# A two-layer hybrid attention trunk: the forget gate's logarithm as a polynomial, a fourth raw weight buffer and four rotary temporaries

## The chip, the core and the metric

The kernel runs on one core of a Trainium2 chip. The metric is device time in microseconds of one execution; times are medians of several runs. Five engines work side by side, each through its own queue of instructions in a fixed order: PE (TensorE, matrix products), ACT (ScalarE, one input and a function from a table), DVE (VectorE, elementwise work on one or two inputs), POOL (GpSimd, a few elementwise steps here) and SP (SyncE, which here only issues transfers). An instruction waits at the head of its queue until its operands are there, and all behind it waits too.

## What is computed

The reference runs two layers and a last RMSNorm on x of 256 positions by 1024 channels, all in fp32. In a layer:

```python
h = rms_norm(x, gain)
proj = h @ w_in                       # 1024 x 9808, split into the parts below
oa = attention_a(rope(qa), rope(ka), va) * silu(ga)         # causal, 8 heads of 64
isc = sum_h w_idx[h] * relu(rope(q_idx)[h] @ rope(k_idx).T) # the indexer
ob = attention_b(rope(qb), rope(kb), vb, top 64 keys of isc) * silu(gb)
log_f = log_sigmoid(f_logit + f_bias)                       # 256 x 8
oc = attention_c(qc, kc, vc, bias = csum(log_f)[t] - csum(log_f)[s]) * silu(gc)
merged = sum_n sigmoid(merge_n) * (o_n @ w_branch[n])
x = x + merged @ w_out
```

The forget gate's `log_f` is the one place that needs a logarithm: with z the logit plus its bias, log_sigmoid(z) = min(z, 0) - log(1 + exp(-|z|)).

## The kernel before, in words

**Weights and precision.** Each product of weights and activations is made of three passes: every operand is split into a high part `hi` (rounded to fp32r) and a remainder `lo`, and PE adds hi·hi, hi·lo and lo·hi. The weights come raw from memory by a transfer on SP into a `raw` buffer of 128 by 2048 (1 MB in all; `R_RAW` = 3 such buffers). From there ACT writes `wh` (L374) and DVE writes `wl` (L378), in pieces of 128 by 1024, into rings of six. A unit of projection work is 24 products of 128 by 256 into one of three `proj` banks (L419), some units in the other orientation with products 512 wide.

**One layer.** First the value projection, then a unit for the indexer's key and the forget logits (`ev_kwf`, `wf_cols`), four indexer units (`index_scores`), and mixer a, between which stand units of the merge gates (L863). After that mixers c and b with the output products, and the last projection. Each rotated projection goes through `rope` (L465): DVE shuffles into a temporary `rsh` (L468), POOL multiplies it by the sine (L469), DVE multiplies the projection by the cosine into `rr` (L470), and POOL adds (L471). There are two `rsh` and two `rr`. From `rr` ACT writes `qh` (L405), DVE the remainder `qy` (L406), and ACT moves three halves into `qx` and `qy` (L591). Then PE makes the scores in two `s` banks (L604 and L606), ACT takes their relu into `tmp` (L818, L819), and DVE adds them up into `isc` (L827, L829). When all four pairs are in, DVE picks 64 keys per row in eight rounds of `MAX` and `MATCH_REPLACE` (L849, L850).

**The forget gate (`wf_cols`, L758).** PE transposes the logits (L763). DVE makes z and -|z| (L772, L773). ACT takes `Exp` (L777) and then `Ln` of e + 1 (L778); the logarithm needs another function table, so an `ACT_TABLE_LOAD` stands in front of it, and another in front of the next function of the first table, the `Tanh` of L863. Then nine small DVE steps on 128 by 16 elements (L782 to L790) correct the logarithm for small e and give `lf`. PE forms the running sum from `lf` (L796, L797), DVE copies it out (L800 to L803), PE transposes (L808), ACT writes `cT` (L810), and SP loads rows of `cT` into `tmp` (L580). These rows are first used by mixer c (L650).

**What sets the order.** All work is entered as operations with a due key, an engine (sometimes a choice of two), a cost and the buffers it needs. `Plan.run` (L143) then plays the list once with those costs and takes on each engine, among what can start first, the operation with the lowest key; a buffer is taken when an operation starts and given back when its last user is done. So the order on every engine follows from the costs and from how many buffers there are: a change of either moves instructions elsewhere too. The plan gives the `Ln` operation 1540 ns, and an empty ACT operation of 1190 ns stands for the second table load:

```python
def ln():
    ACT.activation(e, na, AF.Exp)
    ACT.activation(u, e, AF.Ln, bias=1.0)
act(ln, 0, False, [], [k_lf], key, "ln", 1540.0)
act(lambda: None, 0, False, [k_lf], [], key - 1, "table", 1190.0)
```

Of the kernel before, what the change touches and what calls it, by code (L numbers as in the profile page):

```python
# [9 lines left out]
F32 = mybir.dt.float32  # L10
F32R = mybir.dt.float32r
AF = mybir.ActivationFunctionType
ALU = mybir.AluOpType

L = 2
S = 256
# [11 lines left out]
NR = {"a": 0, "b": 1, "c": 2}  # L28

C_ID, C_UT, C_MASK, C_ROPE, C_END = 0, 128, 256, 512, 1024  # L30
SWAP = list(range(8, 16)) + list(range(0, 8)) + list(range(16, 32))

R_RING = 6
R_RAW = 3
TAIL = {"ACT": 95.0, "DVE": 85.0, "POOL": 0.0, "PE": 0.0, "SP": 0.0}
STEP = 24.0
SPLIT_LEAD = 2.0
# [206 lines left out]
def hybrid_trunk(ctx, tc, x, norm_gain, w_in, forget_bias, w_branch, w_out, final_gain, consts, out):  # L244
    nc = tc.nc
    PE, ACT, DVE, POOL = nc.tensor, nc.scalar, nc.vector, nc.gpsimd
# [22 lines left out]
    def act(fn, n, ps, reads, writes, key, name="", extra=0.0, touch=(), half=False):  # L269
        o = plan.op([("ACT", t_act(n, ps) + extra, fn)], reads, writes, key, 0.0, name, touch)  # L270
        o.half = half
# [51 lines left out]
    k_id, k_rope, k_gT, k_bdz, k_cst, k_fb, k_wf, k_widx, k_lf, k_cs = (Tok() for _ in range(10))  # L323
# [18 lines left out]
    plan.tag("pth", pts[:1])  # L342
    plan.tag("ptl", pts[1:])
    plan.tag("bd", bd)
    for nm, n, cols, dt in (("rsh", 2, S, F32), ("rr", 2, S, F32),
                            ("th", 2, S, F32), ("g", 4, S, F32), ("e", 4, 384, F32), ("st", 8, 8, F32),
                            ("fb", 2, 384, F32), ("ot", 2, S, F32), ("t8", 4, 8, F32), ("mth", MTH, S, F32)):
        tag(nm, n, [128, cols], dt)
# [409 lines left out]
    def wf_cols(l, key):  # L758
        ps = Buf("t")

        def tr():
            for t in range(2):
                PE.transpose(T(ps)[:, t * 16:t * 16 + 16], wf[64:80, t * 128:(t + 1) * 128], ident[64:80, 64:80])  # L763
        pe(tr, 220.0, [k_wf, k_id], [ps], key, "wf")
        v = lambda: T(ps)[:, :32].rearrange("p (t c) -> p t c", t=2)
        sc = float(np.float32(8 ** -0.5 * 64 ** -0.5))
        dve(lambda: DVE.tensor_scalar(widx, v()[:, :, 0:8], sc, None, op0=ALU.mult), 16, [ps], [k_widx], key, "wf")
        z, na, e, u, c, lf = [fz[:, i].rearrange("p (t c) -> p t c", t=2) for i in range(6)]
        fb = fbias[:, l:l + 1, :].to_broadcast([128, 2, 8])

        def pre():
            DVE.tensor_tensor(z, v()[:, :, 8:16], fb, op=ALU.add)  # L772
            DVE.scalar_tensor_tensor(na, z, -1.0, z, op0=ALU.mult, op1=ALU.min)  # L773
        dve(pre, 0, [ps, k_fb], [k_lf], key, "lf", 300.0)

        def ln():
            ACT.activation(e, na, AF.Exp)  # L777
            ACT.activation(u, e, AF.Ln, bias=1.0)  # L778
        act(ln, 0, False, [], [k_lf], key, "ln", 1540.0)
        act(lambda: None, 0, False, [k_lf], [], key - 1, "table", 1190.0)  # L780

        for f in (lambda: DVE.tensor_scalar(c, e, 1.0, None, op0=ALU.add),  # L782
                  lambda: DVE.tensor_scalar(na, c, 1.0, None, op0=ALU.is_equal),
                  lambda: DVE.tensor_scalar(c, c, -1.0, 5e-8, op0=ALU.add, op1=ALU.max),
                  lambda: DVE.reciprocal(c, c),
                  lambda: DVE.tensor_tensor(c, c, e, op=ALU.mult),
                  lambda: DVE.tensor_tensor(u, u, c, op=ALU.mult),
                  lambda: DVE.tensor_tensor(na, na, e, op=ALU.mult),
                  lambda: DVE.tensor_tensor(u, u, na, op=ALU.add),
                  lambda: DVE.scalar_tensor_tensor(lf, z, 0.0, u, op0=ALU.min, op1=ALU.subtract)):  # L790
            dve(f, 0, [], [k_lf], key + 10, "lf", 100.0, port=True)

        cs = Buf("t")

        def cum():
            PE.matmul(T(cs)[:, :16], ut, lf.rearrange("p t c -> p (t c)"), start=True, stop=False)  # L796
            PE.matmul(T(cs)[:, 8:16], ones, lf[:, 0], start=False, stop=True)  # L797
        pe(cum, 400.0, [k_lf, k_cst], [cs], key + 10, "csum", MARGIN)
        w = lambda: T(cs)[:, :16].rearrange("p (t c) -> p t c", t=2)
        dve(lambda: DVE.tensor_copy(csum, w()), 16, [cs], [k_cs], key, "csum")  # L800
        dve(lambda: DVE.tensor_scalar(ncs, w(), -1.0, None, op0=ALU.mult), 16, [cs], [k_cs], key, "csum")
        rep, k_rep = wf.rearrange("p (t r c) -> p t r c", t=2, r=16), Tok()
        dve(lambda: DVE.tensor_copy(rep, w().unsqueeze(2).to_broadcast([128, 2, 16, 8])), S, [cs], [k_rep, k_wf], key + 10, "csum")  # L803
        pt = Buf("t")

        def tr2():
            for t in range(2):
                PE.transpose(T(pt)[:, t * 128:(t + 1) * 128], wf[:, t * 128:(t + 1) * 128], ident)  # L808
        pe(tr2, 225.0, [k_rep, k_id], [pt], key + 10, "cT", MARGIN)
        act(lambda: ACT.activation(cT, T(pt)[:, :S], AF.Copy), S, True, [pt], [k_rep, k_cT], key + 10, "cT")  # L810
# [306 lines left out]
```

## Time and profile before

| | |
|---|---|
| median of 3 runs | 618.05 us (617.97 to 618.89) |
| the profiled execution | 618.74 us |
| its span, first to last instruction | 616.9 us |
| TensorE clock granted | 0.997 of full speed |
| PE / DVE / ACT / POOL busy | 98% / 87% / 73% / 15% of the span |
| moved by transfers | 107.32 MB, mean 174 GB/s |

The span is shorter than the profiled execution by 1.8 us. Times in rows are in us from the span's start. In a row of the timeline the first number is the start and the second the duration; what stands in brackets is the idle time before it and what ended that. Matmuls are pipelined: one lasts 0.28 us, but the next starts 0.11 us after it, so waits of PE are read from the distance between starts and not from its busy share. In a table of stretches each row gives the stretch, its length, and the busy time of PE, its weight loads (PEld), DVE, ACT and POOL with the number of instructions, then the clock, the busy share of the transfer engines and GB/s.

### The profile page before, as it was taken

Reading aid. Unit: us, or ns where it says so; the run is one execution under the profiler, and the core shown is the slowest. Engines: PE = TensorE matmul, PEld = TensorE weight load, DVE = VectorE, ACT = ScalarE, POOL = GpSimd, SP = SyncE. Lnnn points to the kernel's source line nnn. Section 1 sums busy time; section 2 is a strip of 40 time slices with the busy share of each in tenths; the row PEclk is TensorE's granted clock in tenths of the full one; section 3 lists DMA queues with packets and bytes.
Section 4 is the critical chain, followed back from the end, with each engine's and each line's share of the span. In section 5 each row is a group of like instructions: output and inputs, shape, how many; then the busy total and the mean of one; then the engine's idle time right before and its main releaser. Section 6 shows DMA issues by size and latency. Waiting matters only on the chain.

```text
span 616.9 us, 12615 instructions
## 1 busy us (share of the span) xinstructions
PE 606.5 (98%) x4804; PEld 581.1 (94%) x4804; DVE 534.5 (87%) x1322; ACT 451.7 (73%) x948; POOL 95.0 (15%) x101
## 2 busy tenths in 40 slices
PE   8999999999999999999999999999999999999995
PEld 6899999999998999999889999998999989999985
DVE  7899999985998889988588999998678988999773
ACT  5788398876996778775587866997688766987541
POOL 1251242000000233200006305300000013220001
PEclk9999999999999999999999999999999999999998
DMA  8962765655554563575555639455637365453711
GB/s 283 304 195 90 226 171 191 200 171 172 171 173 136 180 197 99 175 237 173 158 170 174 204 114 276 141 170 185 209 103 231 112 201 157 155 169 122 257 35 69
DMA packets 96156, 107.32 MB, mean 174 GB/s; under 512 B 4576, under 2 KB 84832, under 8 KB 96096
## 3 DMA queue, kind: packets, MB, share of 16 engines
q1 hardware_dynamic: 95808, 106.13, 54.7%
q8 instruction: 37, 0.61, 0.4%
q10 hardware_dynamic: 288, 0.39, 0.2%
q14 instruction: 23, 0.19, 0.1%
HBM read 103.37 MB, written 1.05 MB: 169 GB/s over the span
## 4 chain that ended last, share of the span: by engine, by line
PE 78%; DVE 13%; ACT 4%; issue 2%; DMA 1%; POOL 1%; SPq 0%; POOLq 0%; DVEq 0%; ACTq 0%
PE proj L419 68%; DVE wl L378 5%; PE t L692 3%; DVE isc L850 2%; PE proj L996 1%; PE s L604 1%; PE s L606 1%; DVE t L849 1%; DMA x<-in_x_dram 1%; DVE isc L829 1%; DVE rsh L468 1%; ACT wh L374 1%; PE o L708 1%; PE o L711 1%; DVE rr L470 1%
## 5 line engine op out<-in xcount | busy, mean ns | idle before, releaser
L419 PE MATMUL proj<-hTh,wh 128*128 128x256 f32 (+1 forms) x1040 | 270.1, 278 | 0.0
L419 PE MATMUL proj<-hTl,wh 128*128 128x256 f32 (+1 forms) x1040 | 269.7, 277 | 0.0
L378 DVE TENSOR_TENSOR wl<-raw,wh 128x1024 fp32r<-128x1024 f32 (+1 forms) x190 | 235.5, 1248 | 38.3 <-ACT wh L374 37.7
L374 ACT ACTIVATE wh<-raw 128x1024 fp32r<-128x1024 f32 (+1 forms) x190 | 199.0, 1053 | 51.1 <-PE proj L419 41.3
L419 PE MATMUL proj<-hTh,wl 128*128 128x256 f32 (+1 forms) x1040 | 234.0, 278 | 0.0
L419 PEld LDWEIGHTS proj<-hTh,wh 128*128 128x128 f32 (+1 forms) x1040 | 194.7, 187 | 0.2
L419 PEld LDWEIGHTS proj<-hTl,wh 128*128 128x128 f32 (+1 forms) x1040 | 194.6, 187 | 0.3
L419 PEld LDWEIGHTS proj<-hTh,wl 128*128 128x128 f32 (+1 forms) x1040 | 175.6, 187 | 0.0
L469 POOL TENSOR_TENSOR rsh<-rsh,cst 128x256 f32<-128x256 f32 (+1 forms) x42 | 35.6, 849 | 351.9 <-DVE rsh L468 351.7
L471 POOL TENSOR_TENSOR rr<-rr,rsh 128x256 f32<-128x256 f32 (+1 forms) x42 | 51.1, 1220 | 8.2 <-DVE rr L470 5.4
L669 ACT ACTIVATE e<-e,st 128x128 f32<-128x128 f32 x96 | 42.7, 446 | 6.9 <-DVE st L665 6.6
L419 PE MATMUL proj<-wh,v 128*128 128x512 f32 (+1 forms) x144 | 35.5, 368 | 0.0
L419 PE MATMUL proj<-og0l,wh 128*128 128x256 f32 x128 | 33.9, 277 | 0.0
L419 PE MATMUL proj<-og0h,wh 128*128 128x256 f32 x128 | 32.4, 278 | 0.0
L419 PE MATMUL proj<-wh,hTh 128*128 128x512 f32 x80 | 32.4, 405 | 0.0
L419 PE MATMUL proj<-wh,hTl 128*128 128x512 f32 x80 | 31.5, 393 | 0.0
L419 PEld LDWEIGHTS proj<-wh,v 128*128 128x128 f32 x144 | 25.2, 188 | 4.7
L419 PE MATMUL proj<-og0h,wl 128*128 128x256 f32 x128 | 28.6, 277 | 0.0
L697 DVE TENSOR_TENSOR ptl<-t,pth 128x384 fp32r<-128x384 f32 x48 | 24.9, 551 | 0.6 <-ACT pth L695 0.6
L419 PE MATMUL proj<-wl,hTh 128*128 128x512 f32 x80 | 24.9, 392 | 0.0
L419 PEld LDWEIGHTS proj<-og0h,wh 128*128 128x128 f32 x128 | 24.0, 188 | 0.0
L419 PEld LDWEIGHTS proj<-og0l,wh 128*128 128x128 f32 x128 | 24.0, 188 | 0.0
(194 smaller groups left out, 1046.1 us busy)
## 6 DMA issues: line engine op xcount, KB each, us to landing
raw<-in_w_in_dram SPq DMA_DIRECT2D x74, 1024.0 KB, 5.3
raw<-in_w_branch_dram SPq DMA_DIRECT2D x24, 512.0 KB, 3.5
raw<-in_w_out_dram SPq DMA_DIRECT2D x8, 1024.0 KB, 6.9
tmp<-wf SPq DMA_DIRECT2D x16, 128.0 KB, 5.2
raw<-in_w_in_dram SPq DMA_DIRECT2D x3, 512.0 KB, 7.9
x<-in_x_dram SPq DMA_DIRECT2D x4, 256.0 KB, 5.1
raw<-in_w_in_dram SPq DMA_DIRECT2D x2, 320.0 KB, 6.0
out_dram<-tmp SPq DMA_DIRECT2D x2, 320.0 KB, 2.5
```

The lines of the kernel that those rows point to most:

```text
L374: ACT.activation(p[0].v, sel(c.v), AF.Copy)
L378: DVE.tensor_tensor(p[1].v, sel(c.v), p[0].v.bitcast(F32), op=ALU.subtract)
L419: PE.matmul(o(), a(), b(), start=first and i == 0, stop=last and i == n - 1)
L468: dve(lambda: DVE.stream_shuffle(T(sh)[:np_], a(), SWAP), S, [ps], [sh], key, "rope")
L469: gps(lambda: POOL.tensor_tensor(T(sh)[:np_], T(sh)[:np_], s[:np_], op=ALU.mult), S, [k_rope], [sh], key, "rope")
L470: dve(lambda: DVE.tensor_tensor(T(r)[:np_], a(), c[:np_], op=ALU.mult), S, [ps, k_rope], [r], key, "rope")
L471: gps(lambda: POOL.tensor_tensor(T(r)[:np_], T(r)[:np_], T(sh)[:np_], op=ALU.add), S, [sh], [r], key, "rope")
L604: PE.matmul(o.rearrange("p (h c) -> p h c", h=2), qh[:, sl], kl[:, :, :n], start=True, stop=False)
L669: act(lambda t=t, a=a, n=n, e=e, st=st: ACT.activation(T(e)[:, a:a + n], T(e)[:, a:a + n], AF.Exp, bias=T(st)[:, t:t + 1], scale=-1.0, acc ...
L692: PE.transpose(T(ps)[:, i * 128:(i + 1) * 128], T(es[h])[:, i * 128:(i + 1) * 128], ident)
L697: dve(lambda h=h, src=src: DVE.tensor_tensor(T(pl)[:, h], src(), T(ph)[:, h].bitcast(F32), op=ALU.subtract), 384, [ps, kp[h][0]], [kp[h][1 ...
L850: dve(lambda o=o, t8=t8: DVE.match_replace(o, T(t8), o, TAKEN), n, [t8], [k_isc[i]], key + r * step, "top8")
```

## The change

Four things are changed.

1. The logarithm is no longer taken by ACT. With s = e / (e + 2), log(1 + e) = 2 atanh(s), and DVE works out a polynomial in s² with five coefficients: ten steps on 128 by 16 elements (L780 to L789 of the changed kernel) stand for nine. ACT keeps `Exp` alone. The `Ln`, the table load in front of it and the table load behind it go, and so does the plan's empty operation for it.
2. `R_RAW` is 4 and no longer 3.
3. There are four `rsh` and four `rr`, no longer two of each.
4. The room for these, 8 KB and 4 KB per partition, comes from the memory set aside for descriptors of transfers that POOL would issue (`dynamic_dma_scratch_size=1024`); this kernel issues none from POOL.

```diff
+ATANH = (2.0, 0.666663146821, 0.400249102795, 0.279606027472, 0.281783350867)
-R_RAW = 3
+R_RAW = 4
-    for nm, n, cols, dt in (("rsh", 2, S, F32), ("rr", 2, S, F32),
+    for nm, n, cols, dt in (("rsh", 4, S, F32), ("rr", 4, S, F32),
-        def ln():
-            ACT.activation(e, na, AF.Exp)
-            ACT.activation(u, e, AF.Ln, bias=1.0)
-        act(ln, 0, False, [], [k_lf], key, "ln", 1540.0)
-        act(lambda: None, 0, False, [k_lf], [], key - 1, "table", 1190.0)
-
-        for f in (lambda: DVE.tensor_scalar(c, e, 1.0, None, op0=ALU.add),
-                  lambda: DVE.tensor_scalar(na, c, 1.0, None, op0=ALU.is_equal),
-                  lambda: DVE.tensor_scalar(c, c, -1.0, 5e-8, op0=ALU.add, op1=ALU.max),
-                  lambda: DVE.reciprocal(c, c),
-                  lambda: DVE.tensor_tensor(c, c, e, op=ALU.mult),
-                  lambda: DVE.tensor_tensor(u, u, c, op=ALU.mult),
-                  lambda: DVE.tensor_tensor(na, na, e, op=ALU.mult),
-                  lambda: DVE.tensor_tensor(u, u, na, op=ALU.add),
-                  lambda: DVE.scalar_tensor_tensor(lf, z, 0.0, u, op0=ALU.min, op1=ALU.subtract)):
+        act(lambda: ACT.activation(e, na, AF.Exp), 16, False, [], [k_lf], key, "lf")
+
+        s, s2, q = na, c, u
+        for f in (lambda: DVE.tensor_scalar(s2, e, 2.0, None, op0=ALU.add),
+                  lambda: DVE.reciprocal(s2, s2),
+                  lambda: DVE.tensor_tensor(s, e, s2, op=ALU.mult),
+                  lambda: DVE.tensor_tensor(s2, s, s, op=ALU.mult),
+                  lambda: DVE.tensor_scalar(q, s2, ATANH[4], ATANH[3], op0=ALU.mult, op1=ALU.add),
+                  lambda: DVE.tensor_tensor(q, q, s2, op=ALU.mult),
+                  lambda: DVE.scalar_tensor_tensor(q, q, ATANH[2], s2, op0=ALU.add, op1=ALU.mult),
+                  lambda: DVE.scalar_tensor_tensor(q, q, ATANH[1], s2, op0=ALU.add, op1=ALU.mult),
+                  lambda: DVE.scalar_tensor_tensor(q, q, ATANH[0], s, op0=ALU.add, op1=ALU.mult),
+                  lambda: DVE.scalar_tensor_tensor(lf, z, 0.0, q, op0=ALU.min, op1=ALU.subtract)):
             dve(f, 0, [], [k_lf], key + 10, "lf", 100.0, port=True)
...
-    nc = _bacc.Bacc("TRN2", target_bir_lowering=False, num_devices=1)
+    nc = _bacc.Bacc("TRN2", target_bir_lowering=False, num_devices=1, dynamic_dma_scratch_size=1024)
```

Since costs and buffers change, the plan moves instructions on every engine. PE has the same 4145 rows, and they stand as before except in the first part of each layer: rows 169 to about 890, and 2283 to about 2890 (the indexer, mixer a and the start of mixer c). There blocks of 6 to 48 projection products change places with scores, transposes and weighted sums. On SP three raw loads now stand ahead of the first load of `cT` rows in layer 1 that stood behind it, and in layer 2 single row loads stand one or two raw loads later.

ACT in layer 1, from the forget gate's exponential on. Before (`rr` is the rotary sum, `qh` the high part made from it, `acc` the first merge gate):

```order
L777 ACTIVATE fz<-fz 128x16
L778 ACT_TABLE_LOAD
L778 ACTIVATE fz<-fz 128x16
L744 ACTIVATE bd0h<-rr_123 64x256
L374 ACTIVATE wh_68<-raw_118 128x1024
L405 ACTIVATE qh_80<-rr_124 128x256
L374 ACTIVATE wh_63<-raw_118 128x1024
L374 ACTIVATE wh_64<-raw_119 128x1024
L405 ACTIVATE qh_81<-rr_123 128x256
L746 ACTIVATE bd0h<-bd0h 64x256
```

ACT at the same place, after the change:

```order
L777 ACTIVATE fz<-fz 128x16
L745 ACTIVATE bd0h<-rr_126 64x256
L375 ACTIVATE wh_68<-raw_120 128x1024
L375 ACTIVATE wh_63<-raw_120 128x1024
L747 ACTIVATE bd0h<-bd0h 64x256
L406 ACTIVATE qh_80<-rr_127 128x256
L375 ACTIVATE wh_64<-raw_121 128x1024
L592 ACTIVATE qx_83<-qh_80 64x256
L406 ACTIVATE qh_81<-rr_128 128x256
L375 ACTIVATE wh_65<-raw_121 128x1024
L406 ACTIVATE qh_82<-rr_129 128x256
```

The table load and the `Ln` are gone, the rotary sums lie in four buffers (126 to 129) where they lay in two (123, 124), and the three `qh` stand closer together, each still waiting for POOL at the head of ACT's queue. Further down the second table load, ahead of the first `acc`, is gone too.

PE in layer 1 at the indexer's third score (buffers `qh_82`, `qx_85`, `qy_88`). Before:

```order
L419 MATMUL proj_160<-hTl,wh_63 128x256
L419 MATMUL proj_160<-hTh,wl_70 128x256
L419 MATMUL proj_160<-hTh,wh_63 128x256
L419 MATMUL proj_160<-hTl,wh_63 128x256
L419 MATMUL proj_160<-hTh,wh_63 128x256
L419 MATMUL proj_160<-hTh,wl_70 128x256
L419 MATMUL proj_160<-hTl,wh_63 128x256
L604 MATMUL s_162<-bd0l,qh_82 128x256
```

PE at the same place, after the change:

```order
L420 MATMUL proj_165<-hTl,wh_63 128x256
L605 MATMUL s_167<-bd0l,qh_82 128x256
L607 MATMUL s_167<-bd0h,qx_85 128x128
L607 MATMUL s_167<-bd0h,qy_88 128x128
L605 MATMUL s_168<-bd0l,qh_82 128x512
L607 MATMUL s_168<-bd0h,qx_85 128x256
L607 MATMUL s_168<-bd0h,qy_88 128x256
L420 MATMUL proj_165<-hTh,wl_70 128x256
```

The score now stands six products earlier. In layer 1 the first score stands 12 products later, and the running sum of the forget gate 42 later. In layer 2 the third score stands 6 later and the fourth 6 earlier, and the running sum 12 later. The first weighted sum of mixer a in layer 1 stands 6 earlier.

DVE in layer 2 at the end of the forget gate's small steps (`fz`), among the selection rounds. Before:

```order
L789 TENSOR_TENSOR fz<-fz 128x16
L850 MATCH_REPLACE isc<-t_148,isc 128x256
L790 SCALAR_TENSOR_TENSOR fz<-fz 128x16
L378 TENSOR_TENSOR wl_71<-raw_119,wh_64 128x1024
L800 COPY csum<-t_164 128x16
```

DVE at the same place, after the change:

```order
L787 SCALAR_TENSOR_TENSOR fz<-fz 128x16
L849 MATCH_REPLACE isc<-t_153,isc 128x256
L788 SCALAR_TENSOR_TENSOR fz<-fz 128x16
L379 TENSOR_TENSOR wl_70<-raw_118,wh_63 128x1024
L634 SCALAR_TENSOR_TENSOR g_132<-th_130,proj_165 128x256
L789 SCALAR_TENSOR_TENSOR fz<-fz 128x16
L379 TENSOR_TENSOR wl_71<-raw_118,wh_64 128x1024
```

The last `fz` step, for which PE's running sum waits, now stands behind a weight remainder and a gate product of mixer a.

## The prediction

> **What bounds the kernel now.** First the span and the table of stretches, cut where the work of a layer changes: the first part of layer 1, its rest, the first part of layer 2.
>
> ```profile
> span 616.9 us, 12615 instructions
> 31.00:131.00 100.00, 99.45 (x814) 96.10 (x813) 96.60 (x261) 78.60 (x164) 24.49 (x24) 1.00 0.58 181
> 131.00:329.00 198.00, 198.00 (x1547) 188.97 (x1547) 166.20 (x385) 145.07 (x304) 20.25 (x22) 1.00 0.55 173
> 329.00:425.00 96.00, 95.32 (x793) 92.63 (x792) 90.05 (x255) 76.60 (x166) 25.80 (x25) 1.00 0.56 171
> ```
>
> From 131 to 329 PE is busy for every microsecond at full clock. In the two first parts PE is short of that by under 1 us, but DVE is busy for 96.60 of 100 us and 90.05 of 96, and ACT for less than 80%. So the kernel is bound by PE's products, and only in the two first parts does another engine hold PE up. The chain that ended last says the same in shares:
>
> ```profile
> PE 78%; DVE 13%; ACT 4%; issue 2%; DMA 1%; POOL 1%; SPq 0%; POOLq 0%; DVEq 0%; ACTq 0%
> ```
>
> The same chain in order of time, one long piece of projection work, which gives PE's pace:
>
> ```profile
> 128.23 24.52 PE proj L419 x216
> ```
>
> 216 products in 24.52 us are 0.1135 us each. PE's busy share hides short waits, since a product lasts 0.28 us and the next starts after 0.11 us. So I read PE's timeline for starts that lie further apart than that. Here are the seven widest places in the two first parts, with the fourth score of layer 1 (50.90 to 51.29) as the yardstick without a wait:
>
> ```profile
> 47.99 0.28 PE L419 MATMUL proj<-hTl,wh 128*128 128x256 f32 x1
> 48.42 0.27 PE L606 MATMUL s<-bd0h,qy 128*128 128x128 f32 x1
> 49.06 0.50 PE L604 MATMUL s<-bd0l,qh 128*128 128x512 f32 x1 [0.37 <-ACT tmp L819]
> 50.90 0.28 PE L419 MATMUL proj<-hTh,wl 128*128 128x256 f32 x1
> 51.18 0.28 PE L606 MATMUL s<-bd0h,qy 128*128 128x128 f32 x1
> 51.29 0.45 PE L604 MATMUL s<-bd0l,qh 128*128 128x512 f32 x1
> 60.59 0.28 PE L419 MATMUL proj<-hTl,wh 128*128 128x256 f32 x1
> 60.90 0.40 PE L796 MATMUL t<-fz,cst 128*128 128x16 f32 x2
> 85.91 0.28 PE L606 MATMUL s<-bd2h,qy 128*128 128x128 f32 x1
> 86.25 0.50 PE L604 MATMUL s<-bd2l,qh 128*128 128x512 f32 x1
> 98.47 0.28 PE L419 MATMUL proj<-hTl,wh 128*128 128x256 f32 x1
> 98.84 0.36 PE L708 MATMUL o<-pth,v 128*128 128x256 f32 x1
> 340.79 0.28 PE L606 MATMUL s<-bd1h,qy 128*128 128x128 f32 x1
> 341.14 0.50 PE L604 MATMUL s<-bd1l,qh 128*128 128x512 f32 x1
> 345.24 0.22 PE L606 MATMUL s<-bd1h,qx 128*128 128x128 f32 x1
> 345.39 0.33 PE L606 MATMUL s<-bd1h,qy 128*128 128x128 f32 x1
> 345.87 0.50 PE L604 MATMUL s<-bd1l,qh 128*128 128x512 f32 x1
> 360.82 0.28 PE L419 MATMUL proj<-hTl,wh 128*128 128x256 f32 x1
> 361.50 0.40 PE L796 MATMUL t<-fz,cst 128*128 128x16 f32 x2 [0.41 <-DVE fz L790]
> ```
>
> Layer 1: the third score takes 1.07 us from 47.99 to 49.06 against 0.39 on the yardstick, so it waits 0.68; the running sum 0.31 less 0.11, 0.20; the score at 86.25 0.34 less 0.11, 0.23; the weighted sum at 98.84 0.37 less 0.11, 0.26. Layer 2: the second score 0.35 less 0.11, 0.24; the third 0.15 less 0.06 and 0.48 less 0.11, 0.46; the running sum 0.68 less 0.11, 0.57. That is 2.64 us. I take 0.05 more for each restart, since the step after 49.06 is somewhat wider than after 51.29, and so 3.0 us. This is all that a change to order and helpers in these parts can win: 0.5%.
>
> **The change part by part.**
>
> *The table loads.* Two go in each layer.
>
> ```profile
> L778 ACT ACT_TABLE_LOAD x2 | 2.6, 1283 | 0.0
> L863 ACT ACT_TABLE_LOAD x2 | 2.6, 1283 | 0.0
> ```
>
> Two pieces of the chain in order of time, in layer 2:
>
> ```profile
> 341.69 1.28 ACT L863
> 345.34 0.49 ACT tmp L819
> ```
>
> ACT is freed of 2 x 1.28 us and the `Ln` per layer, about 2.7 us. ACT is not what bounds the span, so this counts only where ACT is late for PE. In the chain's order of time the second load of layer 2 (341.69) stands on the chain, ahead of the relu at 345.34 that empties the score bank for the third score. Its 1.28 us are more than the 0.46 that this score waits, and the score stands 6 products (0.68 us) later now. I count the 0.46 whole, between 0 and 0.46. The second score (0.24) lies ahead of that load; only the load after the exponential is out of its way, and there ACT then waits for POOL, so I count 0.14, from 0 to 0.24.
>
> On the cost of a switch, the row says 1.28 us, and the next ACT instruction of the timeline follows at once. The Trainium skill (ScalarE: Activation LUTs, What ACT_TABLE_LOAD costs) puts a drain of about 1.38 us on top, 2.66 us per switch in all; the trace does not agree, since no such gap stands in it, but by that figure ACT would be freed of about 5.3 us per layer.
>
> *The third score of layer 1* now stands 6 products earlier, so PE is there 0.68 us sooner, and the 0.68 that it waited become 1.36 unless ACT comes sooner too. ACT is freed of 2.7 us, but not all arrives: its three `qh` stand at the head of its queue waiting for rotary sums, and POOL now takes the third multiplication ahead of the second sum.
>
> ```profile
> 334.39 0.80 POOL L471 TENSOR_TENSOR rr<-rr,rsh 128x256 f32<-128x256 f32 x1
> 336.94 1.60 POOL L471 TENSOR_TENSOR rr<-rr,rsh 128x256 f32<-128x256 f32 x1
> ```
>
> A sum takes 0.80 or 1.60 us on POOL (layer 2 has both), so one step put ahead delays the second `qh` by 0.8 to 1.6 us. That leaves 1.1 to 1.9 us of the 2.7. I take 1.1, since DVE is nearly always busy here and the longer sum is the usual one in this part; of the 1.36 us some 0.26 remain, and about 0.4 of the 0.68 is won. Bounds: all of it, or -0.68 if nothing arrives.
>
> *The logarithm on DVE.* Ten steps stand for nine per layer.
>
> ```profile
> 45.94 0.17 DVE L782 TENSOR_SCALAR fz<-fz 128x16 f32<-128x16 f32 x1
> 46.14 0.17 DVE L783 TENSOR_SCALAR fz<-fz 128x16 f32<-128x16 f32 x1
> 59.98 0.17 DVE L788 TENSOR_TENSOR fz<-fz 128x16 f32<-128x16 f32 x1
> 60.07 0.29 DVE L849 MAX8 t<-isc 128x8 f32<-128x128 f32 x1
> 361.28 0.16 DVE L790 SCALAR_TENSOR_TENSOR fz<-fz 128x16 f32<-128x16 f32 x1
> 361.36 1.22 DVE L378 TENSOR_TENSOR wl<-raw,wh 128x1024 fp32r<-128x1024 f32 x1
> ```
>
> Two steps behind each other that depend on each other start 0.20 apart (45.94, 46.14); one followed by other work takes 0.09 (59.98, 60.07). In layer 1 six of the nine stood in one row, 6 x 0.20 + 3 x 0.09 = 1.5 us; now nearly all ten stand between other steps, 10 x 0.09 = 0.9. So DVE gains 0.6 us there, and in layer 2, where the nine were partly spread, about nothing; ends, 0.9 saved and 0.5 lost. DVE is nearly always busy, so this is worth having, but the two waits that I ascribe to DVE's pace in mixer a (86.25 and 98.84) come closer as well when PE comes sooner. I count 0 of their 0.49, between -0.5 and +0.49.
>
> *The running sums.* In layer 1 it stands 42 products later, 4.77 us, behind which DVE has some 3.8 us more to do by the rows of the order; the 0.20 goes. In layer 2 it stands 12 later, 1.36 us, but its last `fz` step stands behind a remainder more (1.22) and a gate product (0.3), so DVE must come some 0.7 us sooner than now to keep the wait from growing. I take half of 0.57 as won, 0.28, between -0.5 and +0.57.
>
> *The buffers.* The fourth raw buffer is costed at nothing, and so is the room taken from POOL's descriptors, which no transfer here uses.
>
> ```profile
> ACT wh L374 <- DMA raw<-in_w_in_dram: 6.1, 5, 2.8
> 64.42 1.27 SPq L580 DMA_DIRECT2D tmp<-wf  x2
> 106.33 1.40 DVE L650 SCALAR_TENSOR_TENSOR fb<-tmp,ncs,cst 128x128 f32<-128x128 f32 x4
> ```
>
> ACT waited for raw weights 6.1 us in all, while PE had a ring of six pieces to work on, so no wait of PE goes with it; without that ring up to 2.8 us would show. The row loads for mixer c go out behind three more raw loads on SP's queue, but they left at 64.42 and are first used at 106.33, some 40 us of cover.
>
> *Moved work.* Elsewhere in mixer a blocks change places. Most scores and sums come later, which gives their operands time; the first weighted sum of layer 1 and the fourth score of layer 2 come 6 products earlier. I put 0.2 us against it, from 0 to 1.4.
>
> Sum: 0.46 + 0.14 + 0.40 + 0.20 + 0.28 - 0.20 = 1.28 us, and 0.05 for each of two restarts that go, 1.4 us. The span becomes 615.5 and the profiled execution 617.3; that one lay 0.7 above the median of 618.05, so the median becomes 616.7 us.
>
> **The rivals.**
>
> *Everything clears* (chance 0.17). All seven waits go: 618.05 - 3.0 = 615.0 us. For it: most of the places stand later now. Against: the two at DVE's pace.
>
> *DVE holds the pace* (0.25). ACT's freed time turns into idle time of ACT, PE meets fewer waits at the scores and longer ones at the transposes and weighted sums of mixer a, and the first parts last as long as before: 618.0 us. For it: DVE at 96.60 of 100. Against: in layer 2 DVE has about 6 us of idle time in 96, part of it behind ACT.
>
> *PE comes too soon* (0.14). Four operands come no sooner than before: those of the third score and the first weighted sum in layer 1, of the fourth score in layer 2, and the last `fz` step of layer 2. Three places 6 products earlier cost 0.68 each, the fourth 0.2 more; with 0.46 and 0.20 won at the places that moved back, 618.05 + 2.2 - 0.7 = 619.6 us. It decides where ACT's `qh` come less than 0.68 us sooner; for it, that they wait for POOL at the head of the queue.
>
> *The longer switch* (0.04). If a switch takes ACT longer than its load, twice the time is freed, the third score of layer 1 clears wholly, and so does the second of layer 2: 616.7 - 0.28 - 0.10, 616.3 us. This is what the skill's drain would do; the trace gives no sign of it.
>
> **How the numbers follow.** The forecast has 0.40. A measurement of this kernel tells about 0.2%, 1.24 us, from no change, so faster means below 616.8 and slower above 619.3. The forecast lies almost at that line: 0.25 of it on the faster side, 0.15 on the other. Faster: 0.25 + 0.17 + 0.04 = 0.46. Same: 0.15 + 0.24 of the second rival + 0.02 of the third = 0.41. Slower: 0.12 + 0.01 = 0.13. The range goes from 614.9, just below all waits gone, to 619.0: beyond it lie most of the third rival and a little below, 0.18 together.
>
> **What would show it.** Right: no table load but the first; the relu L819 ahead of the third score of layer 2 at least 0.5 us sooner; starts 0.11 apart at the places of 49.06, 60.90 and 345.87; the stretch of layer 2's first part shorter by 0.7 to 1 us, that of layer 1 by 0.4 to 0.8, and the long middle stretch unchanged. Wrong: the waits found again, as wide, at the transposes (L692) and weighted sums (L708); `qh` waiting longer for POOL; the running sum of layer 2 waiting over 0.6; or a part of the gain or loss outside the first parts of the layers, in the first 31 us above all, where the fourth raw load now leaves earlier beside the others.

## The result, and the profile after

The changed kernel takes 615.07 us (median of 5 runs) against 618.05 us before (5 runs): a ratio of 0.9944, with a 95% interval from 0.9928 to 0.996. It is faster by 3.0 us, about 0.5%. The prediction said 616.7: the gain is more than twice the forecast's 1.4 us. The number is that of the rival in which all seven waits go, 615.0; that it fits to a tenth is in part luck, as the fixed points below show.

The first profile of the changed kernel fell in an execution whose clock was low all through (0.655, a span of 862.4 us), so the profile shown is of another run of the same kernel, `after_again` below. Its span, the stretches that the prediction used, and the shares of the chain that ended last:

```profile
span 612.9 us, 12602 instructions
31.00:131.00 100.00, 100.00 (x829) 97.45 (x828) 96.96 (x263) 79.20 (x168) 21.84 (x24) 1.00 0.58 178
131.00:329.00 198.00, 198.00 (x1547) 188.97 (x1547) 166.89 (x387) 143.60 (x302) 22.13 (x24) 1.00 0.56 176
329.00:425.00 96.00, 96.00 (x793) 93.27 (x792) 93.25 (x259) 75.37 (x161) 22.61 (x24) 1.00 0.57 173
PE 97%; DVE 1%; issue 1%; ACT 0%; POOL 0%; POOLq 0%
```

PE is now busy for every microsecond of the two first parts, where 0.55 and 0.68 us were missing, and within the same 100 us it gets through 829 instructions instead of 814. The chain is PE's at 97% instead of 78%; the 13% that went through DVE are down to 1%, the 4% through ACT to 0%. The middle stretch is as it was. Of ACT's table loads one is left in the whole program:

```profile
L502 ACT ACT_TABLE_LOAD x1 | 1.3, 1283 | 3.6 <-DMA x<-in_x_dram 3.6
```

PE's timeline at three of the seven places: the third score of layer 1 (47.09, the row 512 wide), and the running sums of layer 1 (64.16) and layer 2 (359.26).

```profile
46.98 0.28 PE L607 MATMUL s<-bd0h,qy 128*128 128x128 f32 x1
47.09 0.45 PE L605 MATMUL s<-bd0l,qh 128*128 128x512 f32 x1
...
64.04 0.28 PE L420 MATMUL proj<-hTh,wl 128*128 128x256 f32 x1
64.16 0.29 PE L795 MATMUL t<-fz,cst 128*128 128x16 f32 x2
...
359.14 0.28 PE L420 MATMUL proj<-hTl,wh 128*128 128x256 f32 x1
359.26 0.29 PE L795 MATMUL t<-fz,cst 128*128 128x16 f32 x2
```

Each starts 0.11 or 0.12 us after the row ahead of it; before it was 0.64, 0.31 and 0.68. No wait stands at the other four places either.

To say in which layer the time came, I measure between fixed points. PE transposes the forget logits once in each layer; between these two rows lie all of layer 1's first part and its rest, and from the second to the end of the span lies layer 2. Before:

```profile
27.01 0.29 PE L763 MATMUL t<-cst,wf 16*128 16x16 f32 x2
```

The second such row of before starts at 326.49, those of the changed kernel at 26.43 and 324.24. With spans of 616.94 and 612.89 us, layer 1 goes from 299.48 to 297.81 us (1.67 less), layer 2 from 290.45 to 288.65 (1.80 less), 3.5 us together. The remaining 0.6 of the 4.0 us between the two spans lies ahead of the first transpose and is the profiled execution of before alone: the profiles of all twelve kernels in the table below, that of `poly_old_order` among them, which has before's order, start that row between 26.02 and 26.59.

Over all executions the median span falls by 3.8 us (616.7 for before beside `after_again`, 612.9 for the changed kernel), but the time by only 3.4. The changed kernel spends 2.1 to 2.2 us outside its span in each of its ten executions, and every other kernel of this study 1.7 to 1.9. These 0.35 us are a loss that the prediction did not have, and no run shows what they are; `poly_only` and `buffers_only` have none of it.

### The profile page after: what moved, and what is told of

Its sections match the earlier page's. It is cut to its first block, busy times and chain, and to the rows that moved or that the text cites. A ratio compares the mean times of both kernels' runs of the same rounds, so it can differ in the third digit from the quotient of the medians.

```text
span 862.4 us, 12602 instructions
## 1 busy us (share of the span) xinstructions
PE 854.8 (99%) x4804; PEld 795.8 (92%) x4804; DVE 549.3 (64%) x1324; ACT 454.7 (53%) x941; POOL 90.4 (10%) x102
## 4 chain that ended last, share of the span: by engine, by line
PE 97%; DVE 1%; issue 1%; DMA 0%; POOL 0%; ACT 0%; POOLq 0%; DVEq 0%
PE proj L420 85%; PE t L693 3%; PE s L607 2%; PE s L605 2%; PE proj L995 1%; PE o L709 1%; PE o L712 1%; PE o L710 0%; PE o L711 0%; DMA x<-in_x_dram 0%; PE t L521 0%; PE s L521 0%; DVE wl L987 0%; DVE wh L985 0%; DVE hTl L535 0%
## 5 line engine op out<-in xcount | busy, mean ns | idle before, releaser
L420 PE MATMUL proj<-hTh,wh 128*128 128x256 f32 (+1 forms) x1040 | 349.8, 345 | 0.0
L420 PE MATMUL proj<-hTl,wh 128*128 128x256 f32 (+1 forms) x1040 | 349.3, 344 | 0.0
L420 PE MATMUL proj<-hTh,wl 128*128 128x256 f32 (+1 forms) x1040 | 306.1, 343 | 0.0
L420 PEld LDWEIGHTS proj<-hTl,wh 128*128 128x128 f32 (+1 forms) x1040 | 257.9, 248 | 0.9 <-issue 0.2
L420 PEld LDWEIGHTS proj<-hTh,wh 128*128 128x128 f32 (+1 forms) x1040 | 255.5, 246 | 1.2
L420 PEld LDWEIGHTS proj<-hTh,wl 128*128 128x128 f32 (+1 forms) x1040 | 235.1, 249 | 0.4
L420 PE MATMUL proj<-wh,v 128*128 128x512 f32 (+1 forms) x144 | 48.3, 468 | 0.0
L420 PE MATMUL proj<-og0h,wh 128*128 128x256 f32 x128 | 42.7, 346 | 0.0
L865 ACT ACTIVATE mth<-proj 128x256 f32<-128x256 f32 x32 | 12.3, 383 | 48.5 <-PE proj L420 48.4
L696 ACT ACTIVATE pth<-t 128x384 fp32r<-128x384 f32 x48 | 22.9, 491 | 21.0 <-PE t L693 20.7
```

The source lines that it names most:

```text
L420: PE.matmul(o(), a(), b(), start=first and i == 0, stop=last and i == n - 1)
L696: act(lambda h=h, src=src: ACT.activation(T(ph)[:, h], src(), AF.Copy), 384, True, [ps], [kp[h][0]], key, "pT", touch=[ph])
L865: act(lambda: ACT.activation(T(th), T(ps)[:, :S], AF.Tanh, scale=0.5), S, True, [ps], [th], u - EARLY, "mth")
```

## The experiments

Two theories stood against each other at first. **A**: PE waited for what the two table loads of a layer kept ACT from doing; the order and the buffers matter little. **B**: the new order and the additional buffers removed the waits. All times are medians in us; ratios are to before, run on the same chip beside them (618.47, 618.32 and 618.40 us for the first four kernels, the next four and the last four), with 95% intervals.

| kernel | us | ratio |
|---|---|---|
| `after_again` | 615.04 | 0.9945 (0.9932 to 0.9957) |
| `poly_only` | 615.60 | 0.9953 (0.9940 to 0.9966) |
| `poly_old_order` | 615.40 | 0.9949 (0.9935 to 0.9963) |
| `buffers_only` | 617.14 | 0.9978 (0.9969 to 0.9987) |
| `loads_back` | 618.43 | 1.0003 (0.9994 to 1.0012) |
| `fill_exp` | 615.75 | 0.9961 (0.9948 to 0.9973) |
| `fill_gate` | 618.48 | 1.0000 (0.9992 to 1.0009) |
| `dve_tax` | 621.12 | 1.0050 (1.0037 to 1.0062) |
| `tanh_early` | 616.27 | 0.9963 (0.9950 to 0.9977) |
| `buffers_tanh` | 615.93 | 0.9960 (0.9947 to 0.9972) |
| `poly_raw` | 615.14 | 0.9946 (0.9934 to 0.9958) |
| `poly_temps` | 614.56 | 0.9937 (0.9924 to 0.9949) |

The second table is PE's timeline read as in the prediction: the distance of a start from the one ahead of it, less the pace (0.113 us behind a product 256 wide, 0.06 behind one 128 wide). The seven columns are the places of the prediction: in layer 1 (1) the third score, the running sum, a score and a weighted sum of mixer a, in layer 2 (2) the second score, the third, and the running sum. A dash is less than 0.14 us. These are single distances, so they differ from the prediction's by up to 0.1.

| kernel | 1 third | 1 sum | 1 score a | 1 weighted | 2 second | 2 third | 2 sum |
|---|---|---|---|---|---|---|---|
| before | 0.58 | 0.20 | 0.28 | 0.26 | 0.29 | 0.42 | 0.57 |
| `loads_back` | 0.58 | 0.19 | 0.29 | 0.22 | 0.29 | 0.42 | 0.68 |
| `fill_gate` | 0.59 | 0.17 | 0.28 | 0.17 | - | 0.34 | 0.71 |
| `fill_exp` | - | - | 0.27 | 0.17 | - | - | - |
| `poly_old_order` | - | - | - | 0.18 | - | - | - |
| `tanh_early` | - | - | - | 0.17 | 0.58 | - | - |
| `buffers_only` | - | - | - | - | 0.29 | 0.42 | 0.61 |
| `after_again` | - | - | - | - | - | - | - |

### The parts by themselves

`after_again` is the changed kernel unaltered. `poly_only` has its polynomial with before's numbers of buffers:

```diff
-R_RAW = 4
+R_RAW = 3
-    for nm, n, cols, dt in (("rsh", 4, S, F32), ("rr", 4, S, F32),
+    for nm, n, cols, dt in (("rsh", 2, S, F32), ("rr", 2, S, F32),
```

`buffers_only` is before with the four numbers of the change and its logarithm on ACT kept:

```diff
-R_RAW = 3
+R_RAW = 4
-    for nm, n, cols, dt in (("rsh", 2, S, F32), ("rr", 2, S, F32),
+    for nm, n, cols, dt in (("rsh", 4, S, F32), ("rr", 4, S, F32),
-    nc = _bacc.Bacc("TRN2", target_bir_lowering=False, num_devices=1)
+    nc = _bacc.Bacc("TRN2", target_bir_lowering=False, num_devices=1, dynamic_dma_scratch_size=1024)
```

`poly_old_order` is before with the polynomial in place of the logarithm and nothing else changed: the plan is told the old costs, and two of the ten steps are entered as one operation, so that PE, POOL and SP run word for word in before's order, and ACT does but for the `Ln` and the two loads:

```diff
         def ln():
             ACT.activation(e, na, AF.Exp)
-            ACT.activation(u, e, AF.Ln, bias=1.0)
         act(ln, 0, False, [], [k_lf], key, "ln", 1540.0)
         act(lambda: None, 0, False, [k_lf], [], key - 1, "table", 1190.0)
-        for f in (lambda: DVE.tensor_scalar(c, e, 1.0, None, op0=ALU.add),
...
+        def first():
+            DVE.tensor_scalar(s2, e, 2.0, None, op0=ALU.add)
+            DVE.reciprocal(s2, s2)
+        for f in (first,
+                  lambda: DVE.tensor_tensor(s, e, s2, op=ALU.mult),
...
```

> The changed kernel itself, for a profile at full clock. If all seven waits of the forecast went (the rival in which everything clears), the first part of layer 1 is shorter by 1.3 to 1.5 us and that of layer 2 by 1.3 to 1.5, with starts 0.11 us apart at every one of the seven places; time 0.995 of the kernel before. If the forecast's sum was right part by part and something outside those parts gave the rest, the two first parts are shorter by 1.4 us together, and 1.5 us lie elsewhere, most likely in the first 31 us, where the fourth raw load leaves earlier.

> The polynomial and the plan's new costs, with three raw buffers and two temporaries of each kind as before. Theory A (the time of the table loads on ScalarE is what PE waited for, buffers matter little): faster by 2 to 3 us, ratio 0.995 to 0.997. Theory B (the new order and the buffers that allow it are what clears the waits): faster by 0 to 1 us, ratio 0.998 to 1.000.

> The fourth raw buffer and the four temporaries, with the logarithm from ScalarE's table as before. Theory A: the table loads are still there, so faster by 0.5 us at most, ratio 0.999 to 1.000. Theory B: faster by 1.5 to 2.5 us, ratio 0.996 to 0.998. If PE comes too soon at places moved forward, slower by up to 1 us.

> The polynomial in the order of the kernel before: the plan is given the old costs (the 1540 and the empty 1190 ns) and nine operations for the ten steps, buffers as before, so every instruction stands as it stood and only the Ln and the two table loads per layer are missing. Theory A: faster by 1.5 to 2.5 us, ratio 0.996 to 0.9975, with the waits of layer 1's third score and layer 2's second and third score gone and those of the running sums left. Theory B: faster by under 1 us, ratio 0.9985 to 1.000.

The polynomial alone gives 615.6 us in the order that the plan makes of it and 615.4 in before's own, 2.9 and 3.1 us of the 3.4 that the whole change gives. The old order loses all seven waits but one. Theory A had expected less of it, 1.5 to 2.5 us, with the waits of the running sums left; these go too, and why is shown below. So the order isn't the main cause, and theory B falls as the main one. The buffers alone still give 1.3 us, more than theory A allowed and less than theory B. All of it is in layer 1, which is 1.46 us shorter between the fixed points, while layer 2 is 0.46 longer: they relieve the waits of layer 1 in another way, and so the two gains do not add up.

The order does clear one place that the prediction did not list, because it lies inside a merged row. In layer 2 the second of three transposes of mixer a (387.52 in before) starts 0.32 us after the first, where 0.11 is usual. Every kernel in before's order keeps this wait of 0.2 us, `poly_old_order` too; the changed kernel does not have it.

### Which of the loads, and by what

What of the polynomial was it: the `Ln` no longer waited for, the first load, or the second? `loads_back` puts the instructions back on ACT in `poly_old_order`, but the result of the `Ln` goes to a place that the last small step overwrites, so that it is not used:

```diff
             ACT.activation(e, na, AF.Exp)
+            ACT.activation(lf, e, AF.Ln, bias=1.0)
```

`fill_exp` and `fill_gate` put one idle copy each in the place of one load, behind the exponential or ahead of the layer's first merge gate (`fill` is a buffer of its own that nobody reads):

```diff
             ACT.activation(e, na, AF.Exp)
+            ACT.activation(fill, ident[:, :1].to_broadcast([128, 1280]), AF.Copy)
```

```diff
+            def gate():
+                if late:
+                    late.pop()
+                    ACT.activation(fill, ident[:, :1].to_broadcast([128, 1280]), AF.Copy)
+                ACT.activation(acc[:, j], T(ps)[:, :S], AF.Tanh, scale=0.5)
```

> The polynomial in the order of before, with ScalarE's Ln put back although nobody reads its result: it is written where the last small step writes later. So both table loads of a layer and the Ln come back at their old places on ScalarE, while VectorE keeps the polynomial, which does not wait for the Ln. poly_old_order took 615.4 us, before 618.5. Theory A (PE waited for what the loads kept ScalarE from doing): all of it is lost again, 617.8 to 618.6 us, with PE's waits back at the third score of layer 1 (0.5 us or more) and at the third score of layer 2 (0.4 or more). Rival B (VectorE gained, because its steps no longer wait for a logarithm and stand less in a row): it stays within 0.5 us of 615.4.

> The polynomial in the order of before, with one ScalarE copy of 128 by 1280 (an estimated 1.28 us, by 1056 ns for 1024 columns) right behind the forget gate's exponential, at the place of the first table load; nothing reads it. Theory A as the prediction had it (behind the exponential ScalarE waits for POOL's rotary sums anyway, so the first load mostly fills a wait): 615.4 to 616.0 us. Rival C (ScalarE is in debt through this whole part, so each load costs the same wherever it stands): half of the 3 us, 616.6 to 617.2.

> The polynomial in the order of before, with the same copy of 128 by 1280 on ScalarE in front of the first merge gate of each layer, at the place of the second table load. Theory A as the prediction had it (the second load stands right ahead of the relus for the third score): most of the 3 us comes back, 617.0 to 618.0 us, with the third scores of both layers waiting again. Rival C (each load costs the same): 616.6 to 617.2, as fill_exp.

`loads_back` is before again, in its time and in all seven waits: the gain is ACT's time and nothing that the polynomial does on DVE. And the two loads are not alike. The copy in the first place costs 0.35 us, which the two intervals do not tell from nothing; between the fixed points it is 0.35 in layer 1, where the score of mixer a waits again, and nothing in layer 2. The copy in the second place costs 3.1 us, all of the gain and more than theory A expected. Rival C, the same cost anywhere, falls.

The reason for the first stands on ACT's timeline of layer 1. `poly_old_order` behind its exponential (27.37):

```profile
27.37 0.21 ACT L778 ACTIVATE fz<-fz 128x16 f32<-128x16 f32 x1
29.10 0.42 ACT L745 ACTIVATE bd0h<-rr 64x256 fp32r<-64x256 f32 x1 [1.51 <-POOL rr L472]
```

`fill_exp` there:

```profile
27.81 0.21 ACT L780 ACTIVATE fz<-fz 128x16 f32<-128x16 f32 x1
27.93 1.26 ACT L781 ACTIVATE fill<-cst 128x1280 f32<-128x1280 f32 x1
29.54 0.42 ACT L747 ACTIVATE bd0h<-rr 64x256 fp32r<-64x256 f32 x1 [0.35 <-POOL rr L474]
```

ACT has a hole of 1.51 us there, in which it waits for POOL's rotary sum, and 1.26 us of copy fit into it: the hole becomes 0.35. The second load meets no hole. Before, layer 1:

```profile
40.11 1.28 ACT L863 ACT_TABLE_LOAD   x1
41.41 0.38 ACT L863 ACTIVATE acc<-proj 128x256 f32<-128x256 f32 x1
41.69 1.06 ACT L374 ACTIVATE wh<-raw 128x1024 fp32r<-128x1024 f32 x1
42.64 0.37 ACT L818 ACTIVATE tmp<-s 128x256 f32<-128x256 f32 x1
42.90 0.42 ACT L405 ACTIVATE qh<-rr 128x256 fp32r<-128x256 f32 x1
...
46.76 1.05 ACT L374 ACTIVATE wh<-raw 128x1024 fp32r<-128x1024 f32 x1
47.71 0.37 ACT L818 ACTIVATE tmp<-s 128x256 f32<-128x256 f32 x1
48.11 0.41 ACT L591 ACTIVATE qy<-qh 64x256 fp32r<-64x256 f32 x1
48.43 0.57 ACT L819 ACTIVATE tmp<-s 128x512 f32<-128x512 f32 x1
```

From the load to the relu at 48.43, which empties the score bank for PE's third score (49.06), no row has a bracket: ACT never waits, and so the 1.28 us arrive there whole. `fill_gate` has the same picture with a copy, and PE's third score behind it waits for the same relu:

```profile
39.38 1.25 ACT L874 ACTIVATE fill<-cst 128x1280 f32<-128x1280 f32 x1
40.66 0.39 ACT L875 ACTIVATE acc<-proj 128x256 f32<-128x256 f32 x1
```

```profile
47.66 0.28 PE L609 MATMUL s<-bd0h,qy 128*128 128x128 f32 x1
48.31 0.50 PE L607 MATMUL s<-bd0l,qh 128*128 128x512 f32 x1 [0.37 <-ACT tmp L827]
```

Behind the same load DVE waits too, and this is the part that I had not seen. DVE's timeline of before, all of its waits from 38 to 62 and from 338 to 362:

```profile
43.35 0.42 DVE L406 TENSOR_TENSOR qy<-rr,qh 128x256 fp32r<-128x256 f32 x1 [0.73 <-ACT qh L405]
47.85 1.23 DVE L378 TENSOR_TENSOR wl<-raw,wh 128x1024 fp32r<-128x1024 f32 x1 [0.61 <-ACT wh L374]
...
343.71 0.43 DVE L406 TENSOR_TENSOR qy<-rr,qh 128x256 fp32r<-128x256 f32 x1 [0.23 <-ACT qh L405]
344.65 1.22 DVE L378 TENSOR_TENSOR wl<-raw,wh 128x1024 fp32r<-128x1024 f32 x1 [0.52 <-ACT wh L374]
348.09 1.23 DVE L378 TENSOR_TENSOR wl<-raw,wh 128x1024 fp32r<-128x1024 f32 x1 [0.60 <-ACT wh L374]
```

That is 1.34 us in layer 1 and 1.35 in layer 2, each time behind a `qh` or `wh` that follows the load on ACT (in layer 1 those at 42.90 and 46.76 above). In `poly_old_order` no row of DVE in these two windows has a bracket; in `fill_gate` there are 0.98 and 0.83 us again. Behind them DVE has no wait of 0.1 us or more up to 100 in layer 1 and up to 390 in layer 2, so it carries the delay on to the running sum, for which PE waits 0.57 us in layer 2, and to the score of mixer a in layer 1, which `fill_gate` brings back (0.28).

### Is DVE the pace?

`dve_tax` adds two products to DVE in each layer of `poly_old_order`, behind the second and the sixth small step:

```diff
             DVE.reciprocal(s2, s2)
+            DVE.tensor_tensor(fill[:, :1024], ident[:, :1].to_broadcast([128, 1024]), ident[:, :1].to_broadcast([128, 1024]), op=ALU.mult)
...
             DVE.tensor_tensor(q, q, s2, op=ALU.mult)
+            DVE.tensor_tensor(fill[:, :1024], ident[:, :1].to_broadcast([128, 1024]), ident[:, :1].to_broadcast([128, 1024]), op=ALU.mult)
```

> The polynomial in the order of before, with two more VectorE products of 128 by 1024 in each layer, behind the second and behind the sixth small step; nobody reads them. By the rows of the weight remainders 1.22 us each, 2.4 us per layer, about as much as ScalarE lost with the loads. If VectorE sets PE's pace in the first part of layer 1 (97 of 100 us busy), what it has to do more shows in full there, 2.4 us, and in part in layer 2: 618 to 620 us. If its waits were ScalarE's in the main, it has room: 615.4 to 616.5.

With 621.12 us it lies above both expectations. Against `poly_old_order` it costs 5.7 us, more than the 4.7 that the products take (two groups of 2.4 and 2.3 us). Between the fixed points layer 1 is 3.02 us longer than in `poly_old_order` and layer 2 2.03. In layer 2 that is nearly the 2.4 us of DVE work, and it shows as one wait: the running sum starts 2.01 us after the product ahead of it. In layer 1 the same sum starts 1.68 us after it, so some 0.8 of the 2.4 us were absorbed, but a slower clock was added, which the last section shows. So DVE has under 1 us to spare in each of these parts, and is next to PE's limit; in the kernel before it was held up by ACT.

### The same gain with the logarithm kept

If only the place of the second load counts, it can be moved. `tanh_early` is before with one more instruction, a tiny `Tanh` behind the `Ln`, whose result is overwritten unread, so that the load comes there and not at the merge gate; `buffers_tanh` does the same in `buffers_only`:

```diff
             ACT.activation(u, e, AF.Ln, bias=1.0)
+            ACT.activation(lf, e, AF.Tanh)
```

> The kernel before, with its Ln and its nine steps, and one more ScalarE instruction: a Tanh on 128 by 16 elements right behind the Ln, whose result nobody reads. It calls the second table load there, where ScalarE then waits for POOL's rotary sums, and the merge gates find their table loaded; the order on the other engines is that of before. If the place of the second load is the cause (fill_exp cost 0.35 us, fill_gate 3.1), nearly all of the 3 us is won without the polynomial: 615.4 to 616.6 us. If ScalarE's time counts wherever it is, or two loads in a row outrun the wait for POOL (1.5 us), it stays at 617.5 or above.

> The buffers without the polynomial (buffers_only, 617.14 us), and the same early Tanh behind the Ln. If the polynomial is worth no more than its table loads, this comes near the changed kernel: 615.0 to 616.0 us, a form that keeps the logarithm on ScalarE. If the polynomial wins by itself, it stays above 616.3.

One line wins 2.1 us of the 3.4. Between the fixed points layer 1 is then as short as in `poly_old_order`; what is left is 0.43 us in layer 2, where the two loads and the two small functions take 3.0 us in a row. ACT still waits for POOL behind them, so it isn't that the hole is too short. `tanh_early`, ACT, DVE and then PE:

```profile
327.12 1.28 ACT L779 ACT_TABLE_LOAD   x1
...
333.28 0.42 ACT L405 ACTIVATE qh<-rr 128x256 fp32r<-128x256 f32 x1 [1.08 <-POOL rr L471]
...
338.56 0.57 ACT L820 ACTIVATE tmp<-s 128x512 f32<-128x512 f32 x1
```

```profile
329.61 1.22 DVE L378 TENSOR_TENSOR wl<-raw,wh 128x1024 fp32r<-128x1024 f32 x1 [2.04 <-ACT wh L374]
```

```profile
338.55 0.27 PE L606 MATMUL s<-bd1h,qy 128*128 128x128 f32 x1
339.19 0.50 PE L604 MATMUL s<-bd1l,qh 128*128 128x512 f32 x1 [0.36 <-ACT tmp L820]
```

Between the loads and the hole stands a `wh`, and DVE waits 2.04 us for it (0.27 in `poly_old_order`). Behind that wait stand DVE's next rotary steps, from these POOL makes its next sum, and ACT gets the `qh` at 333.28 half a microsecond later than in `poly_old_order`, counted from the fixed point. The relu at 338.56 is later by as much, and the second score waits 0.58 us for it, twice as long as before; the third score and the running sum don't wait. With the buffers too (615.93) it is not told apart from `tanh_early`; the changed kernel is faster than both by 0.9 us or more, which is below the 1.24 that the prediction took as the bound.

### Which of the buffers

`poly_raw` is the changed kernel with two `rsh` and two `rr`, `poly_temps` the changed kernel with three raw buffers:

```diff
-    for nm, n, cols, dt in (("rsh", 4, S, F32), ("rr", 4, S, F32),
+    for nm, n, cols, dt in (("rsh", 2, S, F32), ("rr", 2, S, F32),
```

```diff
-R_RAW = 4
+R_RAW = 3
```

> The changed kernel with two rsh and two rr: the polynomial and the fourth raw buffer. poly_only took 615.6 us, the changed kernel 615.04. If the raw buffer gives that half microsecond: 615.0 to 615.2; if the rotary temporaries do: 615.5 to 615.8.

> The changed kernel with three raw buffers: the polynomial and the four rotary temporaries. If the temporaries give the half microsecond: 615.0 to 615.2; if the raw buffer does: 615.5 to 615.8.

Neither pair of expectations holds: `poly_raw` alone (615.14) is as fast as the changed kernel (615.04), as it would be if the raw buffer gave the half microsecond, and `poly_temps` is the fastest of all at 614.56 (614.47 to 614.77), below what was expected of either. In its first parts PE has no wait of 0.14 us or more at a score or a sum, as in the changed kernel, while `poly_raw` has two, 0.32 and 0.28, and `poly_only` two, 0.34 and 0.40. So the temporaries are enough, and the fourth raw buffer has no gain beside them that these runs show. The lead of `poly_temps` over the changed kernel is not in the span (612.8 and 612.9 us, medians) but in the 0.35 us outside it. All this is within 0.6 us; I do not rank the three.

## What the prediction had right, and the step that failed

**What bounds the kernel, and where time is to be won.** Right. The gain lies in the two first parts, the middle stretch did not move, and the seven waits went, with an eighth of 0.2 us at the transposes that was not listed. The ceiling of 3.0 us was somewhat low: the time fell by 3.0 in the first comparison and 3.4 in the second, but the two layers by 3.5 in the traces, of which 0.35 are lost again outside the span.

**The layer's sums.** Forecast 0.7 to 1 us for layer 2 and 0.4 to 0.8 for layer 1; measured 1.80 and 1.67. The direction was right, and the terms that missed were all too small. Between the sum of 1.4 and the 3.0 of all seven waits lie 1.6 us: 0.78 are the waits put down to DVE, 0.28 the third score of layer 1, 0.10 the second score of layer 2, 0.20 the loss by moved work and 0.25 the restarts of the waits that were thought to stay.

**The third score of layer 1, 0.40 of 0.68.** Too small. I took 2.7 us of freed ACT time and subtracted POOL's slower sums, because the three `qh` wait for POOL at the head of ACT's queue. They do, but they stand ahead of the second load, where the first one had been swallowed by the same wait. `fill_exp` and `fill_gate` show it: of the two loads the first brings 0.35 us and the second everything. Behind the second load there is no wait for POOL to subtract; 1.28 us arrive, more than the 0.68. In the changed kernel, counted from the fixed point, PE is there 1.4 us sooner and the relu that it waited for (46.14 against 48.43 in before) 1.7.

**The two waits at DVE's pace, 0 of 0.49, and the running sum of layer 2, 0.28 of 0.57.** This is the step that failed, and the largest part of what is missing. "DVE is nearly always busy" (96.60 of 100 us) was read as DVE's own pace. The 3.4 us in which it was not busy were not asked what they waited for: 1.34 of them, and 1.35 in layer 2, were waits for ACT behind the second load, and they shift all that DVE does afterwards. Three of the four waits that I put down to DVE hung on ACT as much as the scores did. `poly_old_order` clears three of them, and `fill_gate` brings these three back. The fourth, at the weighted sum, it only shortens, from 0.26 to 0.18 us, and `fill_gate` leaves it so: what it waits for there, these runs don't single out. **The running sum of layer 1, 0.20 whole,** had the right number by luck: it was to go because the sum stands 42 products later, but in `poly_old_order` it goes in its old place.

**The third score of layer 2, 0.46 whole.** Right, and by the step that was given: the load stands ahead of the relu without a wait between. **The second score, 0.14 of 0.24.** Right in its cause: the second load does not touch it (`fill_gate`), the first load and the `Ln` together do (`loads_back`, 0.29 us in the second table), a copy of 1.26 us in their place just fits (`fill_exp`), and two loads double it (`tanh_early`), there by way of DVE and POOL. It goes whole, though, not by 0.14.

**The logarithm on DVE, 0.6 us less in layer 1.** It was counted at nothing in the sum, and rightly: `loads_back` has the polynomial and both loads, and is at 1.0003 (0.9994 to 1.0012) of before.

**The buffers at nothing.** Nearly right on top of the polynomial (`poly_only` to the changed kernel, 0.56 us), wrong alone, 1.3 us; what the 0.35 us outside the span come from stays open. **Moved work, 0.2 against.** No such loss was seen.

**The rivals.** "Everything clears" came true, but not for its reason, that most places stand later now: in `poly_old_order` they stand where they stood. "DVE holds the pace" has a true premise, as `dve_tax` shows, and a wrong conclusion, since DVE too was being held up. "PE comes too soon" did not happen: the third score of layer 1 stands six products earlier and does not wait. "The longer switch" falls: the copy of 1.25 us in `fill_gate`, without a switch, costs as much (618.48) as both switches and the `Ln` (618.43). The next ACT instruction also starts 0.02 us behind a load (40.11 and 1.28, then 41.41). The drain that the Trainium skill (ScalarE: Activation LUTs, What ACT_TABLE_LOAD costs) adds to a load is not seen in these runs.

## What to carry to other kernels

In this kernel a stall of one engine cost next to nothing where its queue had a hole close behind it, and arrived in full where it had none, at every engine that waits for that queue. So look from the stall forward to the next wait of the same engine, and subtract no wait that lies ahead of it; and look at what stands between the stall and the hole, since another engine may wait for that. An engine at 97% is not yet the pace: ask first what its last 3% wait for. And a table load can be called early, by a tiny instruction in a place where the engine waits anyway: here one line won two thirds of what the polynomial did.

## What the runs showed of the hardware

**A wait of PE was followed by a slower clock.** PE's timeline of `dve_tax` in layer 1 around the wait, and the table of stretches behind it (the clock is the third number from the end):

```profile
59.40 0.28 PE L422 MATMUL proj<-hTl,wh 128*128 128x256 f32 x1
61.08 0.40 PE L808 MATMUL t<-fz,cst 128*128 128x16 f32 x2 [1.40 <-DVE fz L802]
...
63.23 0.41 PE L422 MATMUL proj<-hTh,wh 128*128 128x256 f32 x1
63.44 0.41 PE L422 MATMUL proj<-hTl,wh 128*128 128x256 f32 x1
```

```profile
59.00:62.20 3.20, 1.80 (x16) 1.60 (x15) 3.20 (x18) 1.71 (x3) 0.00 (x0) 1.00 0.00 0
62.20:65.70 3.50, 3.50 (x19) 3.50 (x18) 2.68 (x6) 0.48 (x2) 0.00 (x0) 0.51 0.00 0
65.70:68.00 2.30, 2.30 (x22) 2.30 (x21) 2.30 (x8) 1.24 (x2) 0.00 (x0) 1.00 0.26 60
```

Products start 1.68 us apart over the wait, and from 1.1 us after its end the clock is at 0.51 for 3.5 us: they start 0.21 us apart instead of 0.11, which is another 1.7 us by the clock (an estimate: 3.5 us at half speed). In layer 2 a wait of 2.01 us at the same place had no such tail. The mean clock of each of the five executions of `dve_tax` lies between 0.992 and 0.995, against 0.997 to 0.999 in `poly_old_order`, so the profiled execution was not alone in this. The Trainium skill (TensorE: Matmul & The Clock Gate, Part 1) describes a clock that is halved after an idle window of about 3.4 us whose phase is free-running. The halved clock and the 3.5 us agree with that, and that one wait of two is hit would fit a free-running phase; that a wait of half such a window is enough is more than it says, and no run here tests it further.
